# A two-block mixer on one Trainium2 core: first rows in place and by token halves, constants behind the first weights, GpSimd tensor work on VectorE

## The chip, the core and the metric

The kernel runs on one core of one Trainium2 chip. The core has five engines that work side by side, each through its own list of instructions in a fixed order: TensorE (PE; its weight loads are shown apart as PEld), VectorE (DVE), ScalarE (ACT), GpSimd (POOL) and SyncE (SP), whose queue here issues every DMA. Engines wait for each other through semaphores. The metric is the device time of one execution in microseconds (us); lower is better.

## The reference, cut to what matters

All data is float32; there are 1024 tokens of width 1024.

```python
for layer in range(2):                                   # first block
    h = rms_norm(x, norm_pre[layer])
    proj = h @ w_in[layer]
    gq, gk, gv, gg, gaf, gab, dq, ..., hq, hzf, hzb, hi, hg = split(proj)
    y_a = gla_branch(gq, gk, gv, gg, gaf, gab, ...)      # gated scan, both directions
    y_b = diff_branch(dq, dk, dv, dg, ...)               # differential attention
    y_c = hgrn_branch(hq, hzf, hzb, hi, hg, ...)         # gated scan, both directions
    x = x + rms_norm(concat(y_a, y_b, y_c) @ w_out[layer], norm_post[layer])
# gla_branch's gates: log_g = log_sigmoid(a @ wa2 + ba) / 16, one per direction
# second block: h and hc are x and 256 context rows, normalised and modulated
p, pc = h @ w_in_2, hc @ w_in_2
o_na = neighbourhood_attention(...)                      # each query: a window and all context
o_dn = gated_delta_rule(..., g = -exp(dn_A_log) * softplus(a + dn_dt_bias))
u_na = (o_na * silu(z_na)) @ w_o_na
u_dn = (rms_norm(o_dn) * silu(z_dn)) @ w_o_dn
y = sigmoid(g_na) * u_na + sigmoid(g_dn) * u_dn
out = x + gate * (y @ w_out_2)
```

## The kernel before, in words

**Projections.** Every float32 operand of a large product is split into a high part, a copy in the type fp32r (`H`, made by ScalarE), and the remainder (`L`, made by VectorE as `raw - H`): `split`, L162 and L163. `Weights` loads a piece of a weight into a `wr` tile (two buffers) and splits it into `wH` and `wL`. A product then takes three matmuls for each pair of 128-row pieces: high by high, high by low, low by high (`proj_cm`, `proj_tm`, both shown as `pj`, L234).

**The start.** `layer` loads eight tiles `x` of 128 tokens (tag `at`, four buffers), `prenorm` squares each on ScalarE with a running sum (L307), takes the root of the mean on GpSimd (`rstd_of`, L282 and L283) and writes the normalised row `hn` on VectorE (L312). `transpose_split` turns each `hn` on TensorE (`tps`, L294) and splits the result into `hH` (L298) and `hL` (L299), one pair for each half of 512 tokens. Then come the projections that the first scan needs: `gqk` (queries and keys, 256 columns, two calls of two halves) and `gf`, the gates: a 32-column product `aT`, four small matmuls `z` (L568), and for each of two directions |z + b| on ScalarE (L569), min(z + b, 0) on VectorE (L570), exp and log1p on ScalarE (L573, L575), a subtraction (L577) and another exp (L578). Constants (`layer_constants`: `lm`, which becomes `lvlmask` on L859, and `bd`, `lq`, `lk`, `lg`; `mod_prepare`: `sc`, `modb`; `rcos`, `rsin`, `nwc`) are loaded in the same stretch. `dnb` (L1275, L1286) is a constant of the second block, exp(dn_A_log), in a small tile that shares its buffers with the gates' bias `ba`.

**The scans.** `scan_levels` runs six times (for each layer once for the GLA heads, twice for HGRN). Its first step makes, for each half of the tokens, two tiles K0 and K1: one addition of 128x256 each on GpSimd (L371, L372) and one multiplication each on VectorE (L373, L374), which the matmuls `psb` (L384) read. Levels then follow with `Qt`, `Kt` (L397 to L400) and `psl` (L407); `scan_finish` runs chunk by chunk (`U`, `bd`, `po`).

**The second block.** `modulated` (L1079) writes and splits the modulated rows, every second split on GpSimd. The delta net goes by four pairs of heads: `solve` (inverse by small matmuls, one transposed copy `sysA` on GpSimd, L1391), `delta_read` (L1511: `qd` = exp(gate) * `qT`, twice a pair, the product on GpSimd; L1347 and L1348 make `A`), `x_chain` (`px`, `pv`, `pS`, `rr`, `vd`, `S`: a serial chain over 16 chunks), and `delta_finish`: the sum of squares `l2r` on VectorE (L1211), its root on GpSimd (L1212, L1213), `o * l2r` on VectorE (L1605), transposes `ht` on TensorE (L1146), and `zl * oT` on GpSimd (L1612). `oz_parts` splits those products for the output projection, every second one on GpSimd. `merge` makes `yt` (L1873 on VectorE, then an addition on GpSimd, L1874), splits it, and multiplies by `w_out_2` (`pf`, L1895; `ff`, L1898 on VectorE, L1899 on GpSimd).

**What sets the order.** The order in each engine's list is fixed when the program is built, by a scheduler that simulates the engines and takes ready instructions by priority (`tc.cur_priority`). Work of a `Filler` (further projections) has a low priority and is handed out in portions (`RATE`) between the steps of a scan. So a moved instruction also changes where its neighbours land. DMAs are issued by the SP queue in its order; they share eight semaphores, so each waits for the one eight places before it.

## Time and profile before

| what | value |
|---|---|
| time, median of 3 runs | 2998.18 us (2996.06 to 3002.55) |
| the profiled execution's own time | 2996.87 us |
| its span in the trace | 2995.1 us |
| instructions in the trace | 55723 |
| PE busy | 2751.5 us, 92% of the span |
| PEld busy | 2342.9 us, 78% |
| DVE busy | 1891.6 us, 63% |
| ACT busy | 1228.9 us, 41% |
| POOL busy | 555.2 us, 19% (682 instructions) |
| mean DMA rate | 98 GB/s |

The span is the time from the first to the last instruction that the profiler saw; the execution's time is 1.8 us longer. A busy share is a mean over stretches with different limits: an engine can be idle most of the time and still set the pace of one stretch. "Idle before" is the time in which an engine stood before an instruction, and the name behind the arrow is what ended that wait.

### The profile page before, as it was taken

To read this page: it belongs to the slowest core of one execution; us is meant where nothing else is said; L and a number is where in the kernel's file an instruction comes from. 1 tells how busy PE (TensorE), PEld (TensorE's weight loads), DVE (VectorE), ACT (ScalarE), POOL (GpSimd) and SP (SyncE) were. 2 spreads that over 40 slices of the span, in tenths; PEclk is the share of its full clock that TensorE was granted. 3 is DMA by queue.
4 is the path that set the end of the run, shared out by engine and by line. 5 is a ranking of instruction groups with operands and counts; after the bars stand their busy time and mean duration, and the time that the engine had idled before them with its cause. 6 is when DMAs were issued, how large, how long until landed. Compare 5 with 4: busy or idle time off the path is not lost. (4 is left out here: it accounts for less than half of the span.)

```text
span 2995.1 us, 55723 instructions
## 1 busy us (share of the span) xinstructions
PE 2751.5 (92%) x21790; PEld 2342.9 (78%) x21790; DVE 1891.6 (63%) x4111; ACT 1228.9 (41%) x2729; POOL 555.2 (19%) x682
## 2 busy tenths in 40 slices
PE   7899889998999998899979899998899899989999
PEld 4788778896868886788968779875776677769889
DVE  4668777767546687766675645767686744346661
ACT  4232234556433322345564443433444433345430
POOL 1001212212100012222121212411422110010042
PEclk9999989998999998899989999998999999989999
DMA  3111122314331111223245534352435261255463
GB/s 112 29 43 36 41 79 79 94 48 120 128 142 30 44 36 41 78 80 102 53 132 160 180 88 135 119 137 57 132 107 145 78 172 45 71 151 149 145 206 97
DMA packets 355887, 293.61 MB, mean 98 GB/s; under 512 B 145798, under 2 KB 303110, under 8 KB 355624
## 3 DMA queue, kind: packets, MB, share of 16 engines
q1 hardware_dynamic: 355624, 290.04, 33.5%
q8 instruction: 172, 2.82, 0.4%
q14 instruction: 91, 0.75, 0.1%
HBM read 198.40 MB, written 74.78 MB: 91 GB/s over the span
## 5 line engine op out<-in xcount | busy, mean ns | idle before, releaser
L163 DVE TENSOR_TENSOR wL<-wr,wH 128x512 fp32r<-128x512 f32 (+1 forms) x259 | 188.4, 733 | 216.5 <-ACT wH L162 213.5
L234 PE MATMUL pj<-wH,hH 128*128 128x256 f32 x1024 | 297.2, 292 | 14.8 <-ACT wH L162 8.5
L234 PE MATMUL pj<-wL,hH 128*128 128x256 f32 x1024 | 296.0, 290 | 1.2 <-DVE wL L163 1.2
L234 PE MATMUL pj<-wH,hL 128*128 128x256 f32 x1024 | 293.6, 288 | 0.0
L162 ACT CAST wH<-wr 128x512 fp32r<-128x512 f32 (+1 forms) x259 | 159.3, 618 | 277.8 <-PE pj L234 167.4
L234 PE MATMUL pj<-H,wH 128*128 128x512 f32 (+1 forms) x592 | 243.9, 414 | 8.8 <-DVE naz L1624 4.5
L234 PE MATMUL pj<-L,wH 128*128 128x512 f32 (+1 forms) x592 | 244.6, 413 | 0.0
L234 PE MATMUL pj<-H,wL 128*128 128x512 f32 (+1 forms) x592 | 244.5, 413 | 0.0
L234 PE MATMUL pj<-hH,wH 128*128 128x512 f32 (+1 forms) x544 | 221.5, 408 | 9.5 <-ACT raw L780 5.6
L234 PE MATMUL pj<-hL,wH 128*128 128x512 f32 (+1 forms) x544 | 222.3, 409 | 0.0
L282 POOL TENSOR_SCALAR rs<-ss 128x1 f32<-128x1 f32 (+2 forms) x190 | 68.9, 362 | 824.8 <-ACT sq L842 353.8
L234 PE MATMUL pj<-hH,wL 128*128 128x512 f32 (+1 forms) x544 | 221.5, 407 | 0.0
L234 PEld LDWEIGHTS pj<-wH,hH 128*128 128x128 f32 x1024 | 197.1, 193 | 20.6 <-ACT wH L162 9.9
L234 PEld LDWEIGHTS pj<-wL,hH 128*128 128x128 f32 x1024 | 197.6, 193 | 5.6 <-DVE wL L163 2.0
L234 PEld LDWEIGHTS pj<-wH,hL 128*128 128x128 f32 x1024 | 197.2, 193 | 2.6 <-issue 0.2
L814 DVE TENSOR_REDUCE nm<-psc 128x1 f32<-128x1024 f32 x128 | 155.6, 1219 | 43.1 <-PE psc L812 42.9
L817 ACT ACTIVATE p<-psc,nm 128x1024 f32<-128x1024 f32 x128 | 142.9, 1116 | 59.4 <-DVE nm L814 36.5
L283 POOL TENSOR_TENSOR rs<-rs,mhalf 128x1 f32<-128x1 f32 (+2 forms) x190 | 147.7, 778 | 15.3
L234 PEld LDWEIGHTS pj<-H,wH 128*128 128x128 f32 (+1 forms) x592 | 112.6, 190 | 35.8 <-DVE naz L1624 4.9
L839 PEld LDWEIGHTS pav<-v,wT 128*128 128x128 f32 x1024 | 132.0, 198 | 10.6 <-ACT wT L835 3.7
L839 PE MATMUL pav<-v,wT 128*128 128x128 f32 x1024 | 136.0, 282 | 2.5 <-ACT wT L835 2.0
L234 PEld LDWEIGHTS pj<-hH,wH 128*128 128x128 f32 (+1 forms) x544 | 101.8, 187 | 40.5 <-ACT raw L780 6.8
(420 smaller groups left out, 7231.5 us busy)
## 6 DMA issues: line engine op xcount, KB each, us to landing
wr<-in_w_in_dram SPq DMA_DIRECT2D x240, 256.0 KB
modw<-in_mod_w_dram SPq DMA_DIRECT2D x48, 256.0 KB
xs<-raw SPq DMA_DIRECT2D x128, 64.0 KB
ksw<-k SPq DMA_DIRECT2D x32, 256.0 KB
wor<-in_w_out_dram SPq DMA_DIRECT2D x16, 512.0 KB
yt<-y SPq DMA_DIRECT2D x16, 512.0 KB
xh<-xh SPq DMA_DIRECT2D x32, 256.0 KB
gd<-gth SPq DMA_DIRECT2D x32, 256.0 KB
```

Source lines behind the costliest of these rows:

```text
L162: nc.scalar.copy(H, raw)
L163: (leng or nc.vector).tensor_tensor(L, raw, H.bitcast(F32), ALU.subtract)
L234: mm = k.nc.tensor.matmul(ps, x, y, start=i == 0, stop=i == len(terms) - 1)
L282: nc.gpsimd.tensor_scalar(r, ssq, scale, EPS, ALU.mult, ALU.add)
L283: nc.gpsimd.tensor_tensor(r, r, k.mhalf[:, :n], ALU.pow)
L814: nc.vector.tensor_reduce(nm, ps, axis=AX.X, op=ALU.max, negate=True)
L817: nc.scalar.activation(p, ps, AF.Exp, bias=nm, accum_out=z)
L839: k.mark = nc.tensor.matmul(po[:, :P], wT[:, kt, :], v[kt][:, vc0:vc0 + P], start=kt == 0, stop=kt == KT - 1)
```

## The change

Three things are edited.

1. **First rows.** In layer 0 the eight x tiles are loaded straight into the tag `in` (ten buffers), which before held the normalised rows, and are normalised there; the squares, of which only the sum is used, go into `at`. Behind the fourth row's load come the gate's small weights (`wa`, `Wa`) and the 128 query columns (`Wq`), which now are a piece of their own; the key columns follow as filler `gk`. The four tiles of a token half are normalised and transposed, then that half of `aT` and of the queries is projected, then the other half.
2. **Constants.** `behind` orders the loads of `lm`, `bd`, `lq`, `lk`, `lg`, `sc`, `modb`, `rcos`, `rsin` and `nwc` after the last weight load so far, and some of the VectorE work on them after the last `hL`. `lm` moves from a `be` buffer to a `tmp` buffer.
3. **GpSimd to VectorE.** The K0 and K1 additions (24 of 128x256), the odd splits of `modulated` (8 of 128x512, 4 of 128x256), `qd` (8 of 128x1024), `zl` (4 of 128x1024), the odd splits of `oz_parts` (4 of 128x1024) and the `yt` additions (16 of 128x512) go from GpSimd to VectorE; `solve`'s transposed copy (5 of 128x1024) goes to ScalarE. GpSimd keeps `rs`, `l2r`, the rope products, `ff`, the fills and a few others.

```diff
 class Weights:
-            nc.sync.dma_start(raw, src[i * P:(i + per) * P, :].rearrange("(k p) n -> p k n", p=P))
+            k.lastw = nc.sync.dma_start(raw, src[i * P:(i + per) * P, :].rearrange("(k p) n -> p k n", p=P))
...
+def behind(k, inst, mark):
+
+    info = mybir.DependencyInfo(mybir.DependencyClass.NoSync, mybir.DependencyReason.DATA)
+    k.tc.add_manual_dep(inst.ins, mark.ins.name, info, reason="constants come after the first rows and weights")
+    return inst
+
+
+def prenorm(k, x, row):
+
+    nc = k.nc
+    jk = k.wk.tile([P, D], F32, tag="at", name="jn")
     ss = k.st.tile([P, 1], F32, tag="ss", name="ss")
-    nc.scalar.activation(h, x, AF.Square, accum_out=ss)
+    nc.scalar.activation(jk, x, AF.Square, accum_out=ss)
     r = rstd_of(k, ss, 1, 1.0 / D, k.st, "rs")
...
+    nc.vector.scalar_tensor_tensor(x, x, r, row, ALU.mult, ALU.mult)
...
 def scan_levels
-        nc.gpsimd.tensor_tensor(p0[:, :, 0, :], pf[:, :, 0, :], pb[:, :, 0, :], ALU.add)
-        nc.gpsimd.tensor_tensor(p1[:, :, 1, :], pf[:, :, 1, :], pb[:, :, 1, :], ALU.add)
+        nc.vector.tensor_tensor(p0[:, :, 0, :], pf[:, :, 0, :], pb[:, :, 0, :], ALU.add)
+        nc.vector.tensor_tensor(p1[:, :, 1, :], pf[:, :, 1, :], pb[:, :, 1, :], ALU.add)
...
 def layer
+        h = k.wk.tile([P, D], F32, tag="in", name="hn")
+        nc.sync.dma_start(h, xin(tt) if l == 0 else k.xh[tt])
...
+        if tt == 3:
+            wa = k.wk.tile([32, 2, P], F32, tag="wa", name="wa")
+            nc.gpsimd.memset(wa, 0.0)
+            nc.sync.dma_start(wa[0:16, 0, :], a["gla_wa2_fwd"][l])
+            nc.sync.dma_start(wa[16:32, 1, :], a["gla_wa2_bwd"][l])
+            Wa = Weights(k, w_in[:, 768:800], 32)
+            Wq = Weights(k, w_in[:, 0:P], P)
...
-    F.add("gf", gla_gates())
-    F.add("gqk", cm_tile(0, 256, [lambda d, s_: nc.scalar.activation(d, s_, AF.Copy, scale=32 ** -0.5), copy]))
+    F.add("gk", cm_tile(P, P, [copy]))
...
-    q, kk = F.need("gqk")
-    fs = F.need("gf")
+    first = (gla_gates(), gla_queries())
+    for half in range(2):
+        for tt in range(half * 4, half * 4 + 4):
+            if l == 0:
+                prenorm(k, hn[tt], row)
+            transpose_split(k, hn[tt], half, tt % 4)
+        k.tc.cur_priority += RATE["low"]
+        for gen in first:
+            next(gen)
+        k.tc.cur_priority -= RATE["low"]
+
+    fs, q = (now(gen) for gen in first)
+    kk, = F.need("gk")
     if l == 0:
         layer_constants(k)
-        nc.sync.dma_start(k.rcos, a["rcos"])
+        behind(k, nc.sync.dma_start(k.rcos, a["rcos"]), k.lastw)
...
-    lm = k.wk.tile([P, 4, P], F32, tag="be", name="lm")
-    nc.sync.dma_start(lm, a["lvlmask"])
-    nc.vector.tensor_copy(k.lvlmask, lm)
+    lm = k.wk.tile([P, 4, P], F32, tag="tmp", name="lm")
+    behind(k, nc.sync.dma_start(lm, a["lvlmask"]), k.lastw)
+    behind(k, nc.vector.tensor_copy(k.lvlmask, lm), k.lastL)
...
 def solve
-    nc.gpsimd.tensor_copy(A, R.rearrange("s c r -> s r c"))
+    nc.scalar.copy(A, R.rearrange("s c r -> s r c"))
...
 def delta_read
-        nc.gpsimd.tensor_tensor(e, e, D_.qT, ALU.mult)
+        nc.vector.tensor_tensor(e, e, D_.qT, ALU.mult)
...
 def merge
-                nc.gpsimd.tensor_tensor(t, t, ut[:, hs], ALU.add)
+                nc.vector.tensor_tensor(t, t, ut[:, hs], ALU.add)
```

The names and lines of the rows below are those of the program that they come from; in the changed kernel the same statement stands 5 to 15 lines further down. Numbers behind a name tell one tile from another; an entry in square brackets names the semaphores waited for.

On the SP queue, from the second weight load of the start on, the kernel before has:

```order
L178 DMA wr<-in_w_in_dram 128x2x256 [waits DMAHW3_49]
L861 DMA bd<-in_bd_dram 128x256 [waits DMAHW4_49]
L863 DMA bd<-in_bd_dram 128x128 [waits DMAHW5_49]
L506 DMA x<-in_x_dram 128x1024 [waits DMAHW6_49,DVE_49]
L873 DMA lq<-in_diff_lq_dram 128x64 [waits DMAHW7_49]
...
L506 DMA x<-in_x_dram 128x1024 [waits DMAHW4_49,DVE_49]
L970 DMA sc<-in_c_dram 128x8x1 [waits DMAHW5_49]
L971 DMA sc<-in_c_ctx_dram 128x8x1 [waits DMAHW6_49]
L506 DMA x<-in_x_dram 128x1024 [waits DMAHW7_49,DVE_49,Activation_49]
```

and the changed kernel, from the first weight load on:

```order
L178 DMA wr<-in_w_in_dram 128x8x32 [waits DMAHW0_49]
L178 DMA wr<-in_w_in_dram 128x4x128 [waits DMAHW1_49]
L508 DMA hn<-in_x_dram 128x1024 [waits DMAHW2_49]
L508 DMA hn<-in_x_dram 128x1024 [waits DMAHW3_49]
L508 DMA hn<-in_x_dram 128x1024 [waits DMAHW4_49]
L508 DMA hn<-in_x_dram 128x1024 [waits DMAHW5_49]
L328 DMA ba<-in_gla_ba_fwd_dram 128x1 [waits DMAHW6_49]
```

The last four rows of x no longer wait for VectorE or ScalarE to release a buffer, only for the DMA eight places ahead; the constants stand behind the key weights.

On VectorE, where the last gate values are made and K0 and K1 follow (`f_377` is the second direction's gate, `f_365` the first's), the kernel before has:

```order
L570 TENSOR_SCALAR f_377<-z_379,ba_375 128x512
L859 CAST lvlmask_525<-lm_526 128x512
L570 TENSOR_SCALAR f_377<-z_383,ba_375 128x512
L360 TENSOR_TENSOR B_920<-B_920,f_365 128x512
L577 TENSOR_TENSOR f_377<-f_377,fe_378 128x1024
L362 TENSOR_TENSOR E_921<-E_921,f_377 128x512
L373 TENSOR_TENSOR K0_928<-cmt_472,f_377 128x256
L374 TENSOR_TENSOR K1_929<-cmt_472,f_365 128x256
```

and the changed kernel (there the gates are `f_442` and `f_430`):

```order
L575 TENSOR_SCALAR f_442<-z_448,ba_440 128x512
L374 TENSOR_TENSOR K0_928<-cmt_472 128x256
L375 TENSOR_TENSOR K1_929<-cmt_472 128x256
L377 TENSOR_TENSOR K1_929<-cmt_472,f_430 128x256
L582 TENSOR_TENSOR f_442<-f_442,fe_443 128x1024
L163 TENSOR_TENSOR wL_617<-wr_614,wH_616 128x512
L376 TENSOR_TENSOR K0_928<-cmt_472,f_442 128x256
L365 TENSOR_TENSOR E_921<-E_921,f_442 128x512
```

The cast of `lvlmask` no longer stands ahead of the last gate value, and of K0 and K1 only one multiplication is left behind the second gate.

On ScalarE, at the same place, the kernel before has:

```order
L575 ACTIVATE fe_378<-fe_378 128x1024
L1286 ACT_TABLE_LOAD
L1286 ACTIVATE dnb_17519<-dnb_17519 128x8
L578 ACTIVATE f_377<-f_377 128x1024
L595 COPY cmt_472<-pj_473 128x512
L162 CAST wH_604<-wr_602 128x512
```

and the changed kernel:

```order
L580 ACTIVATE fe_443<-fe_443 128x1024
L162 CAST wH_616<-wr_614 128x512
L1301 ACT_TABLE_LOAD
L1301 ACTIVATE dnb_17519<-dnb_17519 128x8
L583 ACTIVATE f_442<-f_442 128x1024
L162 CAST wH_622<-wr_620 128x512
```

The exp of `dnb` still stands ahead of the second gate's exp; the high parts of three pieces of the value weights (`wH_604`, `wH_610`, `wH_616`) now stand ahead of it. On TensorE, 18 of the 24 matmuls of the first value tile then stand ahead of the first `psb`, where the kernel before has one.

On VectorE, in the third pair's read beside the second pair's finish (`o_23008`), the kernel before has:

```order
L1211 TENSOR_REDUCE l2r_24798<-sq16_24796 128x16
L1544 SCALAR_TENSOR_TENSOR rr_24908<-px_24902,negd_17524,v_23785 128x64
L1544 SCALAR_TENSOR_TENSOR rr_24910<-px_24903,negd_17524,v_23785 128x64
L1347 TENSOR_TENSOR A_24831<-A_24831,gc_17548 128x1024
L1348 SCALAR_TENSOR_TENSOR A_24831<-A_24831,nmask_17395 128x1024
L1605 TENSOR_TENSOR o_23008<-o_23008,l2r_24798 128x1024
```

and the changed kernel:

```order
L1226 TENSOR_REDUCE l2r_24798<-sq16_24796 128x16
L1526 TENSOR_TENSOR qd_24826<-qd_24826,qT_24146 128x1024
L1559 SCALAR_TENSOR_TENSOR rr_24908<-px_24902,negd_17524,v_23785 128x64
L1559 SCALAR_TENSOR_TENSOR rr_24910<-px_24903,negd_17524,v_23785 128x64
L1362 TENSOR_TENSOR A_24831<-A_24831,gc_17548 128x1024
L1363 SCALAR_TENSOR_TENSOR A_24831<-A_24831,nmask_17395 128x1024
L1620 TENSOR_TENSOR o_23008<-o_23008,l2r_24798 128x1024
L1526 TENSOR_TENSOR qd_24837<-qd_24837,qT_24146 128x1024
```

The two products `qd` have come into VectorE's list, one ahead of `o` and one behind it. On GpSimd they stood around the root `l2r`, which now comes up with no product ahead of it:

```order
L1511 TENSOR_TENSOR qd_24826<-qd_24826,qT_24146 128x1024
L1405 MEMSET Tm_25231 32x16x32
L1406 MEMSET Tm_25231 32x16x32
L1212 TENSOR_SCALAR l2r_24798<-l2r_24798 128x16
L1213 TENSOR_TENSOR l2r_24798<-l2r_24798,mhalf_62 128x16
L1511 TENSOR_TENSOR qd_24837<-qd_24837,qT_24146 128x1024
```

```order
L1247 TENSOR_TENSOR sq16_24026<-q_23942,r2col_17399 128x16x16 x2
L1420 MEMSET Tm_23517 32x16x32
L1421 MEMSET Tm_23517 32x16x32
L1227 TENSOR_SCALAR l2r_24798<-l2r_24798 128x16
L1228 TENSOR_TENSOR l2r_24798<-l2r_24798,mhalf_62 128x16
```

The first of the two fences is the kernel before, the second the changed one: the fill of the next `Tm` has moved behind the root as well.

## Rows read from the trace of the kernel before

**Rows 1.** Windows: length; busy PE, PEld, DVE, ACT, POOL; PEclk; DMA share; GB/s

```profile
0.00:100.00 100.00, 70.19 (x400) 49.53 (x400) 40.96 (x77) 44.05 (x71) 14.77 (x33) 0.91 0.34 94
100.00:200.00 100.00, 96.81 (x889) 84.34 (x885) 68.37 (x116) 30.34 (x61) 0.00 (x0) 1.00 0.14 38
```

**Rows 2.** The same view in windows of five microseconds

```profile
5.00:10.00 5.00, 1.03 (x5) 1.03 (x6) 1.28 (x1) 2.65 (x5) 1.01 (x4) 1.00 0.96 370
85.00:90.00 5.00, 4.18 (x67) 4.02 (x67) 1.95 (x3) 0.54 (x2) 0.47 (x1) 0.50 0.38 106
90.00:95.00 5.00, 5.00 (x29) 4.86 (x29) 4.76 (x9) 3.60 (x6) 1.39 (x2) 0.63 0.26 66
```

**Rows 3.** Timeline of ACT: start, duration, line, operation, idle before and releaser

```profile
29.52 1.06 ACT L307 ACTIVATE hn<-x 128x1024 f32<-128x1024 f32 x1 [2.85 <-DMA x<-in_x_dram]
```

**Rows 4.** Timeline of DVE around 68 us

```profile
68.48 0.43 DVE L859 CAST lvlmask<-lm 128x512 uint8<-128x512 f32 x1 [5.95 <-DMA lm<-in_lvlmask_dram]
68.83 0.74 DVE L570 TENSOR_SCALAR f<-z,ba 128x512 f32<-128x512 f32 x1
```

**Rows 5.** Timeline of the SP queue around 69 us

```profile
69.60 1.29 SPq L1275 DMA_DIRECT2D dnb<-in_dn_A_log_dram  x2
```

**Rows 6.** Timeline of ACT around 81 us

```profile
81.00 1.28 ACT L1286 ACT_TABLE_LOAD   x1 [13.55 <-DMA dnb<-in_dn_A_log_dram]
...
82.41 1.04 ACT L578 ACTIVATE f<-f 128x1024 f32<-128x1024 f32 x1
```

**Rows 7.** Timeline of DVE around 84 us

```profile
84.16 0.84 DVE L373 TENSOR_TENSOR K<-cmt,f 128x256 f32<-128x256 f32 x1
84.92 0.83 DVE L374 TENSOR_TENSOR K<-cmt,f 128x256 f32<-128x256 f32 x1
```

**Rows 8.** Timeline of PE around the stop

```profile
84.49 0.58 PE L234 MATMUL pj<-wH,hH 128*128 128x256 f32 x1 [7.90 <-ACT wH L162]
85.90 3.69 PE L384 MATMUL psb<-cmt,K 32*128 32x64 f32 x64 [0.82 <-DVE K L374]
```

**Rows 9.** What PE waited for over the whole span: total us, times, longest

```profile
PE po L468 <- DVE bd L466: 17.8, 9, 5.0
...
PE psl L407 <- DVE Kt L400: 14.2, 8, 6.9
...
PE ht L1146 <- DVE o L1605: 9.0, 2, 5.9
```

**Rows 10.** Timeline of POOL in the delta net's finish

```profile
2282.06 2.41 POOL L1511 TENSOR_TENSOR qd<-qd,qT 128x1024 f32<-128x1024 f32 x1 [19.92 <-ACT qd L1510]
...
2285.70 1.28 POOL L1212 TENSOR_SCALAR l2r<-l2r 128x16 f32<-128x16 f32 x1
2287.06 2.92 POOL L1213 TENSOR_TENSOR l2r<-l2r,mhalf 128x16 f32<-128x16 f32 x1
2289.95 2.34 POOL L1511 TENSOR_TENSOR qd<-qd,qT 128x1024 f32<-128x1024 f32 x1
```

**Rows 11.** Timeline of DVE at the same place

```profile
2282.91 1.22 DVE L1211 TENSOR_REDUCE l2r<-sq 128x16 f32<-128x1024 f32 x1 [2.56 <-ACT sq L1209]
...
2285.68 1.23 DVE L1348 SCALAR_TENSOR_TENSOR A<-A,nmask 128x1024 f32<-128x1024 f32 x1
2290.02 3.35 DVE L1605 TENSOR_TENSOR o<-o,l2r 128x1024 f32<-128x1024 f32 x1 [3.11 <-POOL l2r L1213]
```

**Rows 12.** Timeline of PE at the same place

```profile
2293.52 1.09 PE L1146 MATMUL ht<-ident,o 128*128 128x128 f32 x4 [5.93 <-DVE o L1605]
```

**Rows 13.** Timeline of DVE in a scan's first step

```profile
325.09 2.06 DVE L374 TENSOR_TENSOR K<-kx,f 128x256 f32<-128x256 f32 x2
...
328.94 0.75 DVE L373 TENSOR_TENSOR K<-kx,f 128x256 f32<-128x256 f32 x2
```

**Rows 14.** Timeline of DVE in the merge

```profile
2884.36 0.68 DVE L163 TENSOR_TENSOR yL<-yt,yH 128x512 fp32r<-128x512 f32 x1
2884.96 1.78 DVE L163 TENSOR_TENSOR wL<-wr,wH 128x512 fp32r<-128x512 f32 x1
```

More of the change, by code (lines that the diff above doesn't have):

```diff
@@ L503, in layer @@
     for tt in range(NT):
[L504 to L513 removed]
+        h = k.wk.tile([P, D], F32, tag="in", name="hn")
+        nc.sync.dma_start(h, xin(tt) if l == 0 else k.xh[tt])
+        if l == 0 and tt == 0:
+            row = row_bcast(k, a["norm_pre"][l], D, k.wk, "in")
+        hn.append(h)
+        if tt == 3:
[5 more added lines that the diff above has]
+            Wq = Weights(k, w_in[:, 0:P], P)
     k.hH = [k.hp.tile([P, KT, 512], F32R, tag="hH", name="hH") for _ in range(2)]
     k.hL = [k.hp.tile([P, KT, 512], F32R, tag="hL", name="hL") for _ in range(2)]
[L516 to L517 removed]
     F = Filler(k.tc, RATE["low"])
@@ L528, in cm_tile, with gla_queries @@
             out.append(t)
+        return out
+    def gla_queries():
+        out = k.wk.tile([P, T], F32, tag="in", name="cmt")
+        for half in range(2):
+            nc.scalar.activation(out[:, half * 512:half * 512 + 512], now(proj_cm(k, Wq, 0, P, half)), AF.Copy, scale=32 ** -0.5)
+            yield
         return out
@@ L550, in gla_gates @@
     def gla_gates():
-        wa = k.wk.tile([32, 2, P], F32, tag="wa", name="wa")
-        nc.gpsimd.memset(wa, 0.0)
-        nc.sync.dma_start(wa[0:16, 0, :], a["gla_wa2_fwd"][l])
-        nc.sync.dma_start(wa[16:32, 1, :], a["gla_wa2_bwd"][l])
-        Wa = Weights(k, w_in[:, 768:800], 32)
         aT = k.wk.tile([32, T], F32, tag="be", name="aT")
         for half in range(2):
-            ps = yield from proj_cm(k, Wa, 0, 32, half)
-            nc.scalar.copy(aT[:, half * 512:half * 512 + 512], ps[:32, :])
+            nc.scalar.copy(aT[:, half * 512:half * 512 + 512], now(proj_cm(k, Wa, 0, 32, half))[:32, :])
+            yield
         fs = []
@@ L627, in beside @@
             yield x
-    q, kk = F.need("gqk")
-    fs = F.need("gf")
+    first = (gla_gates(), gla_queries())
+    for half in range(2):
+        for tt in range(half * 4, half * 4 + 4):
[8 more added lines that the diff above has]
+    kk, = F.need("gk")
     if l == 0:
         layer_constants(k)
-        nc.sync.dma_start(k.rcos, a["rcos"])
-        nc.sync.dma_start(k.rsin, a["rsin"])
+        behind(k, nc.sync.dma_start(k.rcos, a["rcos"]), k.lastw)
+        behind(k, nc.sync.dma_start(k.rsin, a["rsin"]), k.lastw)
     k.nwc = norm_columns(k, l)
@@ L1080, in modulated @@
         H, L = parts(kt)
-        split(k, h.rearrange("p (b e) -> p b e", b=8) if i == 0 else hv, H, L, nc.gpsimd if kt % 2 else nc.vector)
+        split(k, h.rearrange("p (b e) -> p b e", b=8) if i == 0 else hv, H, L)
 def context_norm(k):
@@ L1807, in oz_parts @@
         k.nc.sync.dma_start(t, k.ozd[i][c])
-    split(k, t, H, L, k.nc.gpsimd if c % 2 else k.nc.vector)
+    split(k, t, H, L)
     return H, L
```

49 lines of the change are left out of this document (15 added, 34 removed).

## The prediction

> **What bounds the kernel now.** I read the busy table first (PE 92% of the span, DVE 63%, POOL 19%), then the windows, for the stretches in which PE is not full. The first 100 us are the worst: PE is busy for 70.19, so 29.8 are lost, while the next 100 lose 3.2 [rows 1]. Then I read what PE waited for over the span: DVE's names lead it, and three of its lines lie where the edits are [rows 9]. So the kernel is bound by PE, with gaps; only what closes a gap, or opens one, counts.
>
> The timelines of the start show two gaps. First, PE gets rows late: the eighth row's square starts on ACT at 29.52, after a wait for the load [rows 3], although the DMA engines moved 370 GB/s in a window of the start [rows 2]. The second gap is a chain. `lvlmask` waited 5.95 us for `lm` and ran at 68.48; the last gate value stands behind it on DVE and ended at 69.57 [rows 4]. It frees the small `ba` buffer that `dnb` needs, so `dn_A_log` was issued at 69.60 [rows 5]. ACT waited 13.55 us for it, until 81.00, and only then made the second gate's exp, which ended at 83.45 [rows 6]: landing took 11.4 us from issue. The first high parts of the value weights stood behind that exp, K0 and K1 too; PE stood 7.90 us until 84.49 and 0.82 more until `psb` at 85.90 [rows 7, 8]. It came back at half clock: granted 0.50 in the window from 85, which is the 1.2 GHz level, then 0.63 [rows 2]. The 64 `psb` matmuls end at 89.59 [rows 8].
>
> **Edit 1 and 2, the start.** The four late rows lose their wait for a buffer. Eight rows of 0.52 MB with the norm row and the first weights, some 5.4 MB, take 14.5 us at 370 GB/s [rows 2]; with 3 us before the flow starts, the eighth lands near 17.5 instead of 29.5, a lead of 12 us at most. Of it I keep less, since each row then still goes through square, root, scaling, transposes and two splits, and the query products come between. Replaying the new order by hand with the old durations (a transpose group and its split, products at cold and warm spacing), I get the end of the first key product at 70.8 where PE stopped at 76.6 before, 84.49 less 7.90 [rows 8], the fourth `z` at 64.5, its |z + b| at 66.8 and the last gate value, with no `lvlmask` ahead of it, at 67.6. These are estimates, good to some 4 us.
>
> Then `dn_A_log` is issued at 67.6, not 69.60, and with the same 11.4 us lands at 79.0. ACT's order has not changed there: `dnb`'s exp still stands ahead of the second gate's. So the gate's exp ends near 81.5, 2.0 earlier. K0 and K1 took 0.84 and 0.83 behind it [rows 7]; now the additions and one multiplication are done before, and only one is left, near 0.42 each when nothing stretches it (two took 0.75 [rows 13]). `psb` starts near 82.1 instead of 85.90 and ends 3.7 earlier. And 17 matmuls of the value tile, which followed `psb`, now fill part of the stop. They are worth 0.11 us each at the full-speed pace of 889 in 100 us [rows 1], 0.17 at that of 29 in 5 us while the clock came back [rows 2]: 1.9 to 2.9, I take 2.0. **Sum of the start: -5.7.** Bounds: -2 if only the issue moves and the 17 matmuls are lost again to a cold clock; -11 if the gate's exp comes before PE runs dry, since then the 7.90, the 0.82 and about 2 of the half-clock `psb` go.
>
> The added loads and waits: `Wq` is one piece more, two loads of 0.26 MB (0.7 us each at the rate above) ahead of row five, counted in the 5.4 MB. The constants now queue behind the key weights. What needs them: `lvlmask` first in the levels after `psb`, `rcos` much later; they land before 60 in any case, so I cost that at nothing. If they came later than the first level, the stall would be the old 5.95 [rows 4].
>
> **Edit 3, the delta net's finish.** At the second pair's finish the sum of squares ended on DVE at 2284.13 [rows 11]. POOL was in `qd` from 2282.06 to 2284.47, filled two tiles, and began the root at 2285.70, ended it at 2289.98, and started the other `qd` at 2289.95 [rows 10]. DVE's `o`, freed at 2290.02, then took 3.35 instead of the 1.22 of like instructions, the length of POOL's 2.34 more, and PE waited 5.93 until 2293.52 [rows 10 to 12]. Without the products the root starts at 2284.2. Its first half took 1.28 when DVE ran a two-input multiplication (1.23) from the same instant [rows 10, 11]; the new `qd` on DVE can do the same to it, so I charge 1.2 and 2.9, and the end is at 2288.3. On DVE the new order has 1.2 (`qd`), two small steps (`rr`) and 2.5 (two steps of `A`) between the sum of squares and `o`, which gives about the same. Then `o` ends at 2289.5 instead of 2293.37: -3.9. The first pair has the other 3.1 of the 9.0 [rows 9], and by the same charge 1.9 is saved there. **Sum: -5.8**; bounds 0 (if the chain's own steps end last there) and -9.0.
>
> **The merge.** `yt`'s addition on POOL overlaps `wL` and stretches it from 0.68 to 1.78 [rows 14]. Here PE is near full, but the last of these weights gate the first `pf` products; two stretched splits of 1.1, less what the addition costs DVE itself (0.68, as a like one [rows 14]), give -1.5; bounds 0 and -3.
>
> **The scans.** 24 additions of about 0.42 are 10.1 us more on DVE. Against that, the multiplications beside them shrink: two took 2.06 while POOL added, and 0.75 alone [rows 13], 0.84 instead of 0.42 in GLA [rows 7]. Per step that is +0.8 and -0.4 to -0.65 for each multiplication, near even. PE does wait for DVE in the scans (14.2 for `Kt`, 17.8 for `bd` [rows 9]), so I charge +1; bounds 0 and +10.
>
> **What else moves** (`zl`, odd splits, the transposed copy on ACT): DVE takes, by 0.42, 0.68 and 1.22 for the three sizes [rows 11, 13, 14], 10.1 for the K additions, 9.8 for `qd`, 4.9 for `zl`, 4.9 for the splits of `oz`, 10.9 for `yt` and 7.1 for the modulated splits: 47.7 in all, before the relief of the stretched ones. The part not named above lies beside PE-bound stretches with DVE at two thirds: nothing, with +5 if `zl`, 4 times 1.2 us, gets in front of the chain.
>
> **Sum:** -5.7 - 5.8 - 1.5 + 1 = -12. From the profiled execution's 2996.87 that is 2984.9; the median of the runs, 2998.18, is 1.3 above it, so I say 2986.
>
> **Rivals.** *Larger (chance 0.16).* The row loads give their whole lead, the gate's exp comes in time, and every stretch of DVE by POOL goes: -11, -9.0 and -3 are -23, 2975. For it speaks `o`'s 3.35 [rows 11]; against it ACT's order, which keeps `dnb` ahead. The Trainium skill (SBUF — State Buffer, section "SBUF: two separate sides") says that GpSimd and VectorE share a port pair as an exclusive lock, held for a whole instruction, for VectorE work with two SBUF inputs against GpSimd work that reads SBUF. By that rule all moved products gave DVE its time back, and the sum would go towards this rival; the rows above agree at three places, but PE did not wait at most of them.
>
> *Nothing to measure (0.28).* The stop stays: `dn_A_log` lands as late as before or the fourth `z` slips by the query products, and the filled matmuls are lost to later waits, since every order after 100 us is the scheduler's. Then the start gives 2 and the finish 2: 2994.
>
> *Slower (0.11).* DVE becomes the bound where it sets the pace: 10.1 of additions, 8 `qd` and 4 `zl` of 1.22 (14.6) come onto the chains that PE waits for, 24.7 in all. Less the start and the finish (11.5) that is +13, 3011. It decides once more than half of the moved time lies on these chains. For it: 32 us of PE's waits name DVE in the scans [rows 9]. Against it: the additions replace waits for POOL, and the chain of the delta net has an idle DVE.
>
> **How the numbers follow.** My sum has 0.45, with a range of its own of 2980 to 2992; the rivals have the rest. 2975 to 3000 leaves out half of the larger case and the slower one, 2 in 10. About 0.2%, 6 us, is what a measurement of this kernel can tell from no change: faster means below 2992.2. That holds for the sum, the larger rival and a tenth of the third: 0.64; the same 0.26; slower 0.10.
>
> **What would show it.** Right: the eighth square near 17 to 20; `dn_A_log` issued near 67.6 and ACT still waiting for it, but `psb` from about 82 with value products ahead of it; `o` in the finish at 1.2 and PE's waits for it near 3 instead of 9.0; `wL` at 0.69 in the merge; DVE busy up by 20 to 48. Wrong: PE idle in the first 100 us as large as 29.8, or new PE waits for `Kt`, `K` or `rr` that add up to more than 6 us, or a `zl` that holds DVE until its load lands.

## The result, and the profile after

The change took 2975.73 us (median of 4 runs, 2972.34 to 2978.79) where the kernel before took 2999.33 (4 runs, 2996.06 to 3002.55): a ratio of 0.9921, with an interval of 0.9904 to 0.9938, so 23.6 us less. The forecast was 2986, 12 less, in a range of 2975 to 3000. The sign is right and the time lies in the range, but only 0.7 us above its lower edge, and the gain is nearly twice the forecast.

The profiled execution of the changed kernel took 2972.34 and has a span of 2970.5. Its line of busy times:

```profile
PE 2733.2 (92%) x21790; PEld 2329.8 (78%) x21790; DVE 1902.1 (64%) x4179; ACT 1238.2 (42%) x2734; POOL 447.8 (15%) x609
```

PE does the same 21790 matmuls. POOL gave up 107 us, and DVE took only 10.5 more (1891.6 before), although some 48 us of instructions went to it: what stood beside POOL's work before became shorter by most of that (an estimate, the 48 less the 10.5).

Windows of the changed kernel: the first 100 us, as in [rows 1], and six stages that cover the span. Their borders are instructions found in every trace: the first `psb` of the first HGRN scan, the first tile `hH` of layer 2, block two's first modulated tile `hf`, the first and the third `o` of the delta net's finish. Columns as in [rows 1]: length, busy PE, PEld, DVE, ACT, POOL, granted clock, DMA share, GB/s.

```profile
0.00:100.00 100.00, 74.60 (x468) 56.30 (x469) 44.33 (x89) 46.58 (x76) 14.66 (x29) 0.95 0.33 95
0.00:212.06 212.06, 183.67 (x1521) 150.30 (x1521) 119.97 (x221) 79.91 (x144) 16.58 (x31) 0.97 0.24 65
212.06:845.36 633.30, 582.14 (x3973) 511.34 (x3972) 452.48 (x908) 274.64 (x587) 122.66 (x175) 0.96 0.29 87
845.36:1647.27 801.91, 746.63 (x5405) 645.04 (x5405) 537.76 (x1051) 341.21 (x702) 133.29 (x186) 0.96 0.26 76
1647.27:2136.77 489.50, 443.15 (x4358) 378.04 (x4356) 311.92 (x711) 210.25 (x452) 91.26 (x123) 0.96 0.42 117
2136.77:2402.44 265.67, 248.88 (x2659) 189.71 (x2658) 199.21 (x484) 126.37 (x301) 57.50 (x60) 0.98 0.45 124
2402.44:2970.52 568.08, 528.72 (x3885) 455.40 (x3883) 280.78 (x807) 205.78 (x551) 26.56 (x34) 0.98 0.43 129
```

In the first 100 us PE is busy for 74.60 instead of 70.19, and the next hundred kept what was won (97.01 against 96.81). The length of a stage says where time came from, so the same borders were laid through every trace of this study. Start is the first stage, scans the second and third together (1435.2 is 633.30 + 801.91), block two the fourth, finish the fifth, merge and end the sixth; us:

| kernel | start | scans | block two | finish | end | span |
|---|---|---|---|---|---|---|
| before | 219.3 | 1441.5 | 491.0 | 274.4 | 568.8 | 2995.1 |
| before, again | 219.5 | 1440.8 | 496.2 | 274.2 | 570.1 | 3000.8 |
| change | 212.1 | 1435.2 | 489.5 | 265.7 | 568.1 | 2970.5 |
| change, again | 212.0 | 1431.5 | 495.6 | 268.5 | 570.4 | 2977.9 |
| edits 1 and 2 alone | 213.7 | 1450.3 | 490.9 | 264.2 | 571.3 | 2990.5 |
| edit 3 alone | 220.2 | 1441.9 | 484.1 | 263.2 | 565.7 | 2975.0 |
| `qd` alone | 219.2 | 1441.8 | 486.8 | 266.7 | 573.0 | 2987.4 |
| K additions alone | 218.0 | 1442.0 | 485.9 | 278.0 | 571.1 | 2995.1 |
| `yt` alone | 219.2 | 1445.3 | 493.1 | 277.1 | 567.7 | 3002.4 |
| before, other order | 219.4 | 1446.4 | 484.0 | 273.8 | 569.6 | 2993.1 |
| change, other order | 211.2 | 1447.2 | 490.8 | 269.6 | 569.3 | 2988.1 |
| change, `dnb` early | 211.2 | 1440.3 | 497.1 | 270.5 | 573.1 | 2992.2 |
| change, `dnb` loads late | 206.6 | 1443.3 | 497.3 | 270.6 | 571.8 | 2989.6 |
| edit 3 and own `dnb` | 205.8 | 1437.4 | 490.2 | 262.9 | 571.4 | 2967.7 |

From the two traces of before to the two of the change, the means of the stages fall by 7.4 (start), 7.8 (scans), 1.1 (block two), 7.2 (finish) and 0.2 (end). The finish of the change also holds 56 matmuls of 32x32, about 1 us, that stand in the end before.

**The start, row by row.** ACT's timeline (start, duration, line, operation, idle before and releaser):

```profile
18.83 1.06 ACT L314 ACTIVATE jn<-hn 128x1024 f32<-128x1024 f32 x1
...
77.72 1.28 ACT L1301 ACT_TABLE_LOAD   x1 [8.84 <-DMA dnb<-in_dn_A_log_dram]
...
79.13 1.04 ACT L583 ACTIVATE f<-f 128x1024 f32<-128x1024 f32 x1
```

The SP queue's timeline:

```profile
65.96 1.28 SPq L1290 DMA_DIRECT2D dnb<-in_dn_A_log_dram  x2
```

DVE's timeline, at the start and in the finish:

```profile
65.36 0.41 DVE L374 TENSOR_TENSOR K<-cmt 128x256 f32<-128x256 f32 x1
...
80.20 0.43 DVE L376 TENSOR_TENSOR K<-cmt,f 128x256 f32<-128x256 f32 x1 [9.97 <-ACT f L583]
...
2264.63 1.22 DVE L1226 TENSOR_REDUCE l2r<-sq 128x16 f32<-128x1024 f32 x1 [1.24 <-ACT sq L1224]
2265.77 1.22 DVE L1526 TENSOR_TENSOR qd<-qd,qT 128x1024 f32<-128x1024 f32 x1
...
2267.55 1.23 DVE L1362 TENSOR_TENSOR A<-A,gc 128x1024 f32<-128x1024 f32 x1
2268.81 1.23 DVE L1363 SCALAR_TENSOR_TENSOR A<-A,nmask 128x1024 f32<-128x1024 f32 x1
2270.09 1.23 DVE L1620 TENSOR_TENSOR o<-o,l2r 128x1024 f32<-128x1024 f32 x1
```

PE's timeline, at both places:

```profile
70.28 0.45 PE L387 MATMUL psb<-cmt,K 32*128 32x64 f32 x8
...
80.69 3.26 PE L387 MATMUL psb<-cmt,K 32*128 32x64 f32 x56 [8.35 <-DVE K L376]
...
2138.05 1.27 PE L1161 MATMUL ht<-ident,o 128*128 128x128 f32 x8 [1.09 <-DVE o L1620]
...
2276.27 0.66 PE L1161 MATMUL ht<-ident,o 128*128 128x128 f32 x4
```

The eighth square runs at 18.83, 10.7 earlier than in [rows 3]. `dn_A_log` is issued at 65.96 and not 69.60 [rows 5]; ACT still stands before it, 8.84 us until 77.72, and the second gate's exp still stands behind it. So the stop of PE at `psb` is still there, 8.35 us, only earlier: it ends at 83.95 (80.69 + 3.26) where it ended at 89.59 [rows 8].

**The finish.** POOL's timeline, the two halves of the root:

```profile
2266.01 1.04 POOL L1227 TENSOR_SCALAR l2r<-l2r 128x16 f32<-128x16 f32 x1 [37.09 <-DVE l2r L1226]
2267.13 2.92 POOL L1228 TENSOR_TENSOR l2r<-l2r,mhalf 128x16 f32<-128x16 f32 x1
```

The root now starts as soon as the sum of squares is there, and `o` takes 1.23 instead of 3.35 [rows 11]. From the end of the sum to the end of `o` are 5.47 us (2265.85 to 2271.32); before, 9.24 (2284.13 to 2293.37). What PE waited for over the whole span, as in [rows 9]:

```profile
PE psl L410 <- DVE Kt L403: 20.5, 11, 2.7
PE po L471 <- DVE bd L469: 17.5, 12, 2.8
PE ht L1161 <- DVE o L1620: 1.1, 1, 1.1
```

Of the 9.0 us for `o`, 1.1 are left. But at the second pair PE came for `o` only at 2276.27, 5 us after it was done, and without a wait. A chain as long as before, 9.24, would have ended at 2275.09 (an estimate, from 2265.85), and PE would not have waited for that either. Keep this in mind for the experiments.

### The profile page after: what moved, and what is told of

It reads as the page before. It is cut to its first block, busy times and chain, and to the rows that moved or that the text cites. A ratio compares the mean times of both kernels' runs of the same rounds, so it can differ in the third digit from the quotient of the medians.

```text
span 2970.5 us, 55665 instructions
## 1 busy us (share of the span) xinstructions
PE 2733.2 (92%) x21790; PEld 2329.8 (78%) x21790; DVE 1902.1 (64%) x4179; ACT 1238.2 (42%) x2734; POOL 447.8 (15%) x609
## 4 chain that ended last, share of the span: by engine, by line
PE 50%; DVE 10%; DMA 7%; ACT 3%; issue 3%; POOL 2%; SPq 2%; POOLq 0%; DVEq 0%; ACTq 0%
PE pj L234 24%; PE pout L743 6%; PE pu L234 2%; PE pno L1797 2%; PE pf L1910 2%; PE pav L854 2%; PE ppt L1793 1%; DVE at L419 1%; DVE wL L163 1%; DMA wr<-in_w_in_dram 1%; PE pS L1552 1%; PE psc L827 1%; PE px L1552 1%; PE psc L826 1%; PE pt L849 1%
## 5 line engine op out<-in xcount | busy, mean ns | idle before, releaser
L163 DVE TENSOR_TENSOR wL<-wr,wH 128x512 fp32r<-128x512 f32 (+1 forms) x259 | 179.5, 698 | 193.5 <-ACT wH L162 184.3
L234 PEld LDWEIGHTS pj<-H,wL 128*128 128x128 f32 (+1 forms) x592 | 111.1, 188 | 25.4 <-DVE wL L163 0.6
```

Of the source, the lines that this page charges most:

```text
L163: (leng or nc.vector).tensor_tensor(L, raw, H.bitcast(F32), ALU.subtract)
L234: mm = k.nc.tensor.matmul(ps, x, y, start=i == 0, stop=i == len(terms) - 1)
```

## The experiments

My theory at this point: two stalls gave the gain (start and finish), and the change's other moves cost and bring little. Rivals: that GpSimd's products as a whole had cost VectorE, and through it PE, that much; and that the difference beyond the sum is only the order into which the scheduler put the rest. The baseline's runs on the chips of the studies had medians from 3001.99 to 3004.47; each ratio is against the baseline on the same chip.

**Edits 1 and 2 alone, edit 3 alone.** The first is the changed kernel with edit 3 undone, the second the kernel before with all of edit 3.

Against the change, for each moved operation:

```diff
-        nc.vector.tensor_tensor(e, e, D_.qT, ALU.mult)
+        nc.gpsimd.tensor_tensor(e, e, D_.qT, ALU.mult)
...
```

and against the kernel before:

```diff
-        nc.gpsimd.tensor_tensor(zv, zv, oT.rearrange("p (r b c) -> p b r c", b=8, c=8), ALU.mult)
+        nc.vector.tensor_tensor(zv, zv, oT.rearrange("p (r b c) -> p b r c", b=8, c=8), ALU.mult)
...
```

> The first two edits alone (first rows in place and by halves, constants behind), all GpSimd work where it was. Theory A, the gains are local and add up by place: psb starts near 81 instead of 85.90 and the whole kernel gains 7 to 8 us, near 2991. Theory B, most of the total beyond the start is the scheduler's new order after 100 us: the same lead of 7 to 8 us at 100 us, but the end anywhere between -15 and +3, with layer two and the delta net as far from the kernel before as they are in the changed one.

> The third edit alone: all the moved GpSimd work on VectorE and the copy on ScalarE, the start as before. Theory A: the start as before (psb at 85.9), the rest as in the changed kernel: -15 to -17 us, near 2983, most of it between 2100 and 2400 us, where PE's wait of 9.0 for o goes. Theory C, VectorE's port relief counts in full in the scans as well: -6 in each layer's HGRN scans on top. Theory B: the sum of this and of the start alone is not the change's 23.6, by 6 us or more.

Edits 1 and 2: 2990.16, ratio 0.9954 (0.9942 to 0.9967). Edit 3: 2977.0, ratio 0.9905 (0.9891 to 0.9918), as large as the whole change. They don't add up: 0.9954 times 0.9905 is 0.9859, the change has 0.9921. The table shows why. Edits 1 and 2 shorten the start by 5.7 us, as forecast, and edit 3 leaves it alone. Edits 1 and 2 also lengthen the scans, to 1450.3, where PE is idle for 112.4 us instead of 103.5 and 102.6 before. Both kernels shorten the finish by 10 to 11 us, which can be had only once; and edit 3's shorter block two (484.1) is not there in the change.

PE's timeline at the start, with edits 1 and 2 alone:

```profile
82.58 3.26 PE L387 MATMUL psb<-cmt,K 32*128 32x64 f32 x56 [8.29 <-DVE K L376]
```

That edits 1 and 2 shorten the finish is odd, since they touch nothing there. DVE's timeline with them alone:

```profile
2287.08 1.22 DVE L1226 TENSOR_REDUCE l2r<-sq 128x16 f32<-128x1024 f32 x1 [1.68 <-ACT sq L1224]
...
2294.08 3.42 DVE L1620 TENSOR_TENSOR o<-o,l2r 128x1024 f32<-128x1024 f32 x1 [3.10 <-POOL l2r L1228]
```

and PE's:

```profile
2297.56 1.09 PE L1161 MATMUL ht<-ident,o 128*128 128x128 f32 x8 [0.51 <-DVE o L1620]
```

The chain is as slow as before: 9.2 us from the end of the sum (2288.30) to the end of `o` (2297.50), `o` stretched to 3.42 beside POOL's `qd`. Yet PE waited 0.51, not 5.93 [rows 12]: the scheduler's new order had other matmuls there.

**`qd` alone** moves the delta net's eight multiplications and nothing else.

```diff
-        nc.gpsimd.tensor_tensor(e, e, D_.qT, ALU.mult)
+        nc.vector.tensor_tensor(e, e, D_.qT, ALU.mult)
```

> Only the eight qd products go to VectorE. Theory A as predicted on record: PE's waits for o fall from 9.0 to about 3, -5.8 us, near 2993.5. Theory A with the clock: each PE stop that goes also saves the half-clock stretch behind it, -9 to -12, near 2988 to 2990. Theory D, the gain between 2200 and 2400 comes from several moved products together (zl, the copy in solve) and not from qd: -2 to -4, 2996.

2992.34, ratio 0.9955 (0.9942 to 0.9969). The finish falls by 7.6 us, and PE's waits for `o` to 1.1 here too. POOL's timeline at the second pair:

```profile
2277.71 0.21 POOL L1212 TENSOR_SCALAR l2r<-l2r 128x16 f32<-128x16 f32 x1 [13.05 <-DVE l2r L1211]
2278.00 2.92 POOL L1213 TENSOR_TENSOR l2r<-l2r,mhalf 128x16 f32<-128x16 f32 x1
```

With no DVE instruction beside it the root's first half takes 0.21, against 1.04 beside `qd` in the change; the second takes 2.92 in both. So the charge that I made on the root was real for its first half, 0.8 us.

The chain as a whole is not shorter here. DVE's timeline:

```profile
2276.33 1.22 DVE L1211 TENSOR_REDUCE l2r<-sq 128x16 f32<-128x1024 f32 x1 [1.13 <-ACT sq L1209]
2282.74 1.23 DVE L1511 TENSOR_TENSOR qd<-qd,qT 128x1024 f32<-128x1024 f32 x1 [5.18 <-ACT qd L1510]
...
2285.40 1.22 DVE L1605 TENSOR_TENSOR o<-o,l2r 128x1024 f32<-128x1024 f32 x1
```

and PE's:

```profile
2293.30 0.66 PE L1146 MATMUL ht<-ident,o 128*128 128x128 f32 x4
```

`qd` stands ahead of `o` in DVE's list and waits 5.18 for its exp, so from the end of the sum (2277.55) to the end of `o` (2286.62) are 9.07 us, as before. PE came 6.68 after that and did not wait. At the first pair the chain is short (5.44 us, 2143.55 to 2148.99) and PE waits 1.09.

**K additions alone**, the 24 of the scans:

```diff
-        nc.gpsimd.tensor_tensor(p0[:, :, 0, :], pf[:, :, 0, :], pb[:, :, 0, :], ALU.add)
-        nc.gpsimd.tensor_tensor(p1[:, :, 1, :], pf[:, :, 1, :], pb[:, :, 1, :], ALU.add)
+        nc.vector.tensor_tensor(p0[:, :, 0, :], pf[:, :, 0, :], pb[:, :, 0, :], ALU.add)
+        nc.vector.tensor_tensor(p1[:, :, 1, :], pf[:, :, 1, :], pb[:, :, 1, :], ALU.add)
```

> Only the 24 additions for K0 and K1 go to VectorE. As predicted on record they cost about 1 us, at most 10. Theory A: the gain of 4 to 5 us that each HGRN stage shows in the changed kernel comes from them (the roots of the finish no longer queue behind them on GpSimd): -8 to -10, near 0.997. Theory E: no difference beyond 0.1%.

2994.23, ratio 0.997 (0.9959 to 0.9981). The page's line of busy times:

```profile
PE 2751.8 (92%) x21790; PEld 2341.9 (78%) x21790; DVE 1890.4 (63%) x4135; ACT 1228.2 (41%) x2729; POOL 526.8 (18%) x658
```

DVE has 24 instructions more and is busy for 1.2 us less, which is within what two traces of the kernel before differ by (1891.6 and 1894.7): the additions of 0.42 are paid for by the multiplications beside them. The time is what theory A expected, the place is not: the scans, where the additions stand, are no shorter (1442.0), and what the run gained lies in block two (485.9), where nothing was moved.

**`yt` alone**, the merge's addition:

```diff
-                nc.gpsimd.tensor_tensor(t, t, ut[:, hs], ALU.add)
+                nc.vector.tensor_tensor(t, t, ut[:, hs], ALU.add)
```

> Only the 16 additions of yt go from GpSimd to VectorE; the order on TensorE is that of the kernel before. As predicted on record: wL in the merge at 0.69, -1.5 us, a ratio of 0.9995. Theory F, PE is full there and the merge gained only because a half-clock spell was missing: wL shrinks all the same, the idle time of PE from the first yt to the end stays at 5 to 6 us, no difference beyond 0.1%.

3002.94, ratio 1.0 (0.9987 to 1.0012), with TensorE's order unchanged. The merge's weight splits in the window from 2840 to 2900 us, grouped by line (minimum, median, maximum in ns), with the move and, under "before", without it:

```profile
L163 DVE TENSOR_TENSOR wL<-wr,wH x2: 685/688/691, 2892.7 to 2894.8; 128x512 fp32r<-128x512 f32 x2
```

```profile
L163 DVE TENSOR_TENSOR wL<-wr,wH x5: 691/1171/1784, 2882.7 to 2898.4; 128x512 fp32r<-128x512 f32 x5
```

The stretch is gone, and no change of the time is seen. The interval reaches from 3.9 us less to 3.6 more, so it can't tell the 1.5 of my forecast from nothing; the trace says more. From the first `yt` to the end PE is idle for 6.65 and 6.87 us in the two traces of before, for 6.10 with the move, and for 7.06 and 6.79 in the change: at most some 0.8 us of waiting went, and in the change none.

**Another order, nothing moved.** One number of the scheduler's table makes it place the fill work elsewhere, in the kernel before and in the change:

```diff
-RATE = {... "fin": 1.09 ...}
+RATE = {... "fin": 1.12 ...}
```

> The kernel before with one number of the filler's portions changed (1.09 to 1.12 in the scan's finish). No operation is moved to another engine, only the order of projections between the scans' steps changes. Theory B, order alone moves several us: the HGRN and attention stages and those of the second block each differ by 2 to 7 us from the kernel before, in both directions, and the time by up to 8 us. Theory A: within 2 us everywhere.

> The changed kernel with the same number changed. Theory B: the time differs from the changed kernel's by 3 to 10 us, more likely up than down since the changed kernel's HGRN and attention stages have less half-clock time than any other order measured. The start (-7) and PE's wait for o (1 instead of 9) stay. Theory A: the ratio stays at 0.992 to 0.993.

The kernel before: 2997.1, ratio 0.9976 (0.9962 to 0.9989). The change: 2987.28, ratio 0.9935 (0.9919 to 0.9952). So an order alone, with the same instructions, is worth 0.24%, nearly what the K additions "gave", and at the same place: block two falls to 484.0. There the traces fall into two groups, near 484 to 487 (order of before changed, K, `qd`, edit 3) and 489 to 497 (the rest), and no edit decides which. PE's waits for `o` stay in the reordered kernel before:

```profile
PE ht L1146 <- DVE o L1605: 9.1, 2, 6.2
```

The first group is more than noise: PE is idle for 39.5 to 40.1 us of block two in its four traces, and for 45.8 to 47.0 in the two traces each of before and of the change.

In the change the other order's trace lacks the scans' gain (1447.2, against 1435.2 and 1431.5) and keeps the start's (211.2). But that trace is the slowest of six executions (2980.01 to 2990.0), the interval of the ratio overlaps with the change's, and PE's idle time is nearly the same (237.1, against 237.3 and 233.9 in the change). So it is not shown that this order is slower than the change's.

**Both kernels once more**, unchanged, in a later series:

```diff
 (no edit)
```

> The kernel before once more, for a second trace. If the half-clock spells of PE belong to the kernel's order, idle time and half-clock time by stage repeat within about 2 us a stage. If they fall by chance, stages of the second block differ from the first trace by 5 us or more with the order unchanged.

> The changed kernel once more. The ratio comes out at 0.992 again; its trace shows which of the stage gains repeat. Theory A: the start (-7), the HGRN stages (-5 each) and the finish (-9) repeat within 2 us each. Theory E, half-clock spells are chance: the part of a stage's gain that is half-clock time does not repeat, the part that is idle time does.

Before: 3002.62 in one execution. The change: 2981.68, ratio 0.993 (0.9913 to 0.9948), 20.7 us less. The stages repeat within some 6 us, and the scans' shorter time is there in both traces of the change. How the whole gain splits into PE's idle and busy time does not repeat: idle falls by 6.3 and busy by 18.3 in the first pair of traces (busy 2751.5 to 2733.2, each span less its busy time), by 17.5 and 5.4 in the second (2749.4 to 2744.0). I therefore read lengths of stages first; in the scans by themselves the split does repeat (below).

**The stop of the start, taken away.** Two kernels give `dnb` a tile of its own, so that its loads wait for no buffer, and put its exp behind the first gate's exp. In the second the loads stand behind that of `rsin` in the queue.

```diff
-        t = k.st.tile([P, 8], F32, tag="ba", name="dnb")
+        t = k.st.tile([P, 8], F32, tag="dnb", name="dnb", bufs=2)
...
-    nc.scalar.activation(al, al, AF.Exp)
+    behind(k, nc.scalar.activation(al, al, AF.Exp), k.gate0)
```

and in the second also

```diff
...
-            nc.sync.dma_start(t[h * 64:h * 64 + 64, :], src[:, h].partition_broadcast(64))
+            behind(k, nc.sync.dma_start(t[h * 64:h * 64 + 64, :], src[:, h].partition_broadcast(64)), k.rsinld)
```

> The changed kernel with a small tile of its own for dnb, so that its loads are issued near 15 us, and its exp ordered behind the first gate's exp. If what is left of the stop hangs on that load alone, PE's wait of 8.35 us for K ahead of psb goes, psb starts near 70.5 and runs at full clock, and the kernel gains 8 to 11 us on the changed one, near 2966. If another late step takes its place (the key weights behind four more loads on the queue, the table loads on ScalarE), the gain is 0 to 4.

> The changed kernel with a small tile of its own for dnb, its four loads ordered behind rsin (after the constants, so the key weights don't wait behind them), its exp behind the first gate's exp. PE's wait of 8.35 us for K ahead of psb goes, psb starts near 70.5 and the scan's first step runs at full clock: -8 to -11 us on the changed kernel at the second scan, as much at the end if nothing later takes it back, a ratio near 0.989. If the lead of the start is lost later, as it seems to be between the start alone and the moves alone, the end is within 3 us of the changed kernel.

Early: 2992.31, ratio 0.9957 (0.9944 to 0.9969); late loads: 2991.41, ratio 0.9952 (0.9937 to 0.9968). Both came out slower than the change (2981.68 on the chip of the second), though the intervals of the ratios touch its 0.9913 to 0.9948. With the early loads a new stop takes the place of the old. The SP queue's timeline:

```profile
18.49 1.28 SPq L1292 DMA_DIRECT2D dnb<-in_dn_A_log_dram  x2
19.90 14.41 SPq L178 DMA_DIRECT2D wr<-in_w_in_dram  x3
```

ACT's:

```profile
32.57 0.62 ACT L162 CAST wH<-wr 128x512 fp32r<-128x512 f32 x1 [12.02 <-DMA wr<-in_w_in_dram]
```

and PE's:

```profile
34.53 1.06 PE L234 MATMUL pj<-hH,wH 128*32 128x512 f32 x2 [12.54 <-ACT hH L298]
```

The row of 14.41 us merges three issues, the third of which waits for a free buffer. The first weight piece, issued at 19.90 behind `dnb`'s loads, was there only at 32.57, 12.7 us later; in the change it is issued at 15.19 and split at 20.35 without a wait. ACT waited 12.02 for it, the rows' `hH` stands behind that split in its list, and PE stood 12.54 for `hH`, where it stood 0.68 in the change. With the late loads, ACT's timeline has the next one to be late:

```profile
56.78 0.20 ACT L895 ACTIVATE ls<-ls 128x2 f32<-128x2 f32 x1 [9.63 <-DVE ls L894]
```

ACT waits 9.63 (5.02 in the change) for a constant that now lies behind `dnb` in the queue. Even so `psb` runs without the stop, its first 8 at 76.89 and the others here:

```profile
78.88 1.79 PE L387 MATMUL psb<-cmt,K 32*128 32x64 f32 x56
```

The start is 5.5 us shorter than the change's (206.6 against 212.1), and everything after it 24.6 us longer (spans less starts, 2783.0 against 2758.4), in all four stages, or 17.0 against the change's second trace (2766.0). Nothing there was edited, and nothing there was reordered either: in both kernels with an own `dnb` tile the instructions of PE, DVE and POOL stand in the change's order, name by name, and those of ACT too but for `dnb`'s exp.

**Edit 3 with a `dnb` of its own**, put on the kernel before: the lines of edit 3 and those of the last kernel together, without edits 1 and 2.

```diff
-        t = k.st.tile([P, 8], F32, tag="ba", name="dnb")
+        t = k.st.tile([P, 8], F32, tag="dnb", name="dnb", bufs=2)
...
-        nc.gpsimd.tensor_tensor(e, e, D_.qT, ALU.mult)
+        nc.vector.tensor_tensor(e, e, D_.qT, ALU.mult)
...
```

> The third edit alone, with a small tile of its own for dnb, loaded behind rsin, its exp behind the first gate's exp. ACT's wait of 13.55 us goes; psb starts near 74 instead of 85.9, the second gate's exp now waiting for lvlmask's place in VectorE's list only. If nothing takes that back: -8 to -11 on the third edit alone, a ratio near 0.987, better than the change. Theory B: anything from 0.985 to 0.993.

2973.09, ratio 0.9899 (0.9882 to 0.9917). PE's timeline at `psb`:

```profile
75.61 2.01 PE L391 MATMUL psb<-cmt,K 32*128 32x64 f32 x64
```

No wait, and 2.01 us for the 64 matmuls that took 3.69 after the stop [rows 8]. It is the best version of the study; its interval overlaps with those of the change and of edit 3 alone, so that it beats the kernel before is shown, that it beats the change is not.

## Why the prediction was right, and where its sizes were off

**The start, -5.7: right, and by its steps.** The eighth square ran at 18.83 (17 to 20 forecast); `dn_A_log` was issued at 65.96 (67.6) and landed 11.8 later (11.4), with ACT still waiting for it; the gate's exp was done at 80.17 (81.5), with one K multiplication of 0.43 behind it and 18 value products and part of `psb` ahead of the stop. The sum was 3.7 for the end of `psb` and 2.0 for those products. With edits 1 and 2 alone `psb` ends at 85.84, 3.75 earlier than the 89.59 of [rows 8], and the stage is 5.6 to 5.8 shorter: the forecast. In the change `psb` ends 5.64 earlier, 1.3 us of it because the gate's exp was done ahead of its forecast, and the stage is 7.4 shorter. That `dnb` keeps its place ahead of the gate's exp was the argument against the larger rival, and it held; the time came out at that rival's 2975, but not by its mechanism.

**The finish, -5.8: PE's wait went, but at the second pair not because of the shorter chain.** At the first pair the wait fell from 3.09 to 1.09, 2.0 less (1.9 forecast). At the second pair the chain became 3.77 shorter (3.9 forecast), and I expected a wait of about 2 to stay. None did, because PE now came for `o` 10.42 us after the sum of squares, where it had come 3.46 after it (2293.52 less 5.93, less 2284.13): other matmuls stood ahead. That hides a chain of the old length as well. `qd` alone has a chain of 9.07 there and no stop, edits 1 and 2 alone one of 9.20 and a stop of 0.51. So the step that failed is that PE would come for `o` when it came before, and the size came out near by luck. In all eight traces with `qd` on DVE that stop is gone; of the six with `qd` on POOL five keep it, at 5.9 to 6.7. So the move may well be what makes the scheduler put other work there, but no run shows why it does.

There was also more to save than the idle time that I counted. PE's timeline of the kernel before, behind the stop of [rows 12]:

```profile
2295.26 0.63 PE L234 MATMUL pj<-H,wL 128*128 128x512 f32 x1
2295.68 0.63 PE L234 MATMUL pj<-H,wH 128*128 128x512 f32 x1
...
2299.17 0.40 PE L234 MATMUL pj<-H,wH 128*128 128x512 f32 x1
2299.40 0.40 PE L234 MATMUL pj<-L,wH 128*128 128x512 f32 x1
```

Matmuls start 0.42 to 0.43 apart and later 0.23. From 2294.83 to 2298.67 nine of them have the long distance, some 0.2 us too long each, 1.8 us on top of the 5.93. Windows of that place in the kernel before (columns as in [rows 1]) show the granted clock behind the stop, between its levels of 1.2 GHz (0.50) and 2.4 GHz (1.00):

```profile
2290.00:2295.00 5.00, 1.48 (x6) 1.42 (x7) 4.98 (x3) 0.48 (x2) 2.29 (x1) 0.69 0.96 244
2295.00:2300.00 5.00, 5.00 (x16) 3.92 (x15) 3.81 (x5) 3.03 (x7) 0.00 (x0) 0.63 0.51 194
```

In the change, where PE came to `o` without a stop, it is 1.00 throughout:

```profile
2275.00:2280.00 5.00, 5.00 (x83) 4.23 (x83) 4.93 (x5) 2.56 (x4) 0.00 (x0) 1.00 1.00 285
```

I counted such a stretch for the start and forgot it here.

**The merge, -1.5: not seen.** `yt` alone came out at 1.0, which can't tell 1.5 us from nothing. The stretched splits were there and went, but PE's idle time behind them fell by 0.8 at most, and in the change not at all.

**The scans, +1: right in that the additions cost nothing.** With them alone DVE was busy for 1890.4 against 1891.6, and the multiplications fell to 0.42 as forecast. DVE's rise of 10.5 in all is below my 20 to 48: the relief that I left out of the 47.7 was larger. The slower rival never came near.

**What the sum left out.** The step that failed is the last of the sum: that the parts not named give "nothing". The scans became 7.8 us shorter, a third of the gain, with no stall removed there. Windows over the scans (columns as in [rows 1]), in the kernel before, the change, the change again, and the change with `dnb` loads late:

```profile
219.28:1660.82 1441.54, 1338.09 (x9378) 1164.39 (x9377) 989.58 (x1945) 616.83 (x1288) 274.10 (x377) 0.96 0.28 81
212.06:1647.27 1435.21, 1328.77 (x9378) 1156.37 (x9377) 990.24 (x1959) 615.85 (x1288) 255.96 (x361) 0.96 0.28 81
211.97:1643.48 1431.51, 1328.15 (x9378) 1157.40 (x9377) 990.36 (x1960) 614.77 (x1288) 255.36 (x361) 0.96 0.28 81
206.59:1649.87 1443.28, 1338.91 (x9378) 1167.27 (x9377) 989.95 (x1959) 615.14 (x1288) 255.01 (x361) 0.96 0.28 81
```

PE's idle time did not fall (103.5 before, 106.4 and 103.4 in the change). The same 9378 matmuls took 9.3 and 9.9 us less of busy time: their pace was higher. The granted clock rounds to 0.96 in all four, but it stood at 0.50 for 122.9 and 126.3 us in the two traces of the kernel before, for 109.2 and 105.8 in those of the change, and for 122.8 with `dnb` late, where the gain is gone although the instructions stand in the change's order. So the scans' gain is neither the additions (1442.0 alone), nor the new start (1450.3 alone, longer), nor the order by itself; the change ran its scans with more of the full clock, in both traces, and which timing brings that is open.

Together: -7.4 and -7.2 where I had -5.7 and -5.8, and -9.1 in the other three stages, where I had -0.5 for the merge and the scans. Without the scans' 7.8 the time would be near 2983 (an estimate), inside the 2980 to 2992 of my sum. That it came to 2975 is luck, as far as this prediction goes. The rival that GpSimd's products as a whole had cost PE that much is not borne out where it was tried apart (the scans at 1442.0 with the K additions alone, 1.0 for `yt`), though edit 3 as a whole gives as much alone as the change.

It also stays open by which instructions one order is better than another: the waits that head the list are no shorter in the change (`Kt` 20.5 against 14.2 [rows 9], `bd` 17.5 against 17.8).
